# Key and query pieces of the attention layer: one product of 512 columns for the upper weights, and a sum afterwards

## The chip, the core and the metric

The kernel runs on one core of a Trainium2 chip. The core has a matrix engine (TensorE, PE in the profile, with its weight loads as PEld), a vector engine (VectorE, DVE), an activation engine (ScalarE, ACT), a general engine (GpSimd, POOL) and DMA queues, here issued from SyncE (SP). The time is the device time of one execution in microseconds (us); lower is better.

## The reference

A two-layer encoder trunk over 256 tokens of width 2048 in float32. Layer 0 mixes tokens with a convolution module, layer 1 with latent attention; each is followed by an MLP of width 8192. The change lies in the attention of layer 1:

```python
def mla(h, cos, sin, w_in, q_norm_g, kv_norm_g, w_q_up, w_kv_up, w_o):
    down = h @ w_in
    c_q, c_kv, k_pe = jnp.split(down, [Q_LORA_RANK, Q_LORA_RANK + KV_LORA_RANK], axis=-1)   # 512, 512, 64
    q = (rms_norm(c_q, q_norm_g) @ w_q_up).reshape(B, S, N_HEADS, QK_NOPE_DIM + QK_ROPE_DIM)
    q_nope, q_pe = jnp.split(q, [QK_NOPE_DIM], axis=-1)              # 128, 64 for each of 16 heads
    kv = (rms_norm(c_kv, kv_norm_g) @ w_kv_up).reshape(B, S, N_HEADS, QK_NOPE_DIM + V_HEAD_DIM)
    k_nope, v = jnp.split(kv, [QK_NOPE_DIM], axis=-1)                # 128, 128
    ...   # rotary parts, masked softmax of (q_nope k_nope + q_pe k_pe) * scale, times v
    return o @ w_o
```

## The kernel before

**Precision by parts.** A float32 operand is split into an upper part (a copy to a shorter float format, `fp32r`) and a lower part (the operand minus its upper part). A product is three matmuls that add up in one PSUM tile: upper times upper, lower times upper, upper times lower. ACT makes every upper part, DVE nearly every lower part, so each split is an ACT instruction followed by a DVE instruction that waits for it. Weights are split this way after each load (`split_half`, L164 to L179: ACT L170, DVE L174), one half of a unit at a time.

**Attention.** `kvh`/`kvl` and `qh`/`ql` hold the two parts of the normed compressed key/value and query, turned so that the 512 compressed channels lie on partitions in four blocks (`j` of `NJ` = 4) and the 256 tokens are columns. They are made by `to_T` from `ckv` and `cq` (ACT L209, DVE L216), for the query after `squares` (ACT L1502) and `normed` (DVE L1508). The 16 heads come in four groups of four. Work of a group is cut into pieces:

- `k_piece` and `qn_piece` (four of each in a group, one for each head): 12 matmuls of 256 columns, L1535 to L1537 and L1564 to L1566, into one PSUM tile, then `in_parts`: ACT makes the upper part (L209) and DVE the lower part (L214) of the 128 x 256 result, both from PSUM.
- `v_piece` (four): six matmuls of 512 columns; DVE copies the finished tile (L1552).
- `qp_piece` (two): the rotary part of the query; ACT copies it (L1579), POOL rotates it (`rope`, L1380 to L1385), and a few pieces later ACT and POOL split it (`qp_parts`: ACT L209 writing `qhl`, POOL L1599). `qp_turn` transposes it on PE (L1606), and ACT copies it out (L1615, L1616).

For each head, `scores` multiplies query and key parts on PE (10 matmuls), DVE takes the row maximum (L1651, L1652), ACT the exponential (L1654), and `weights` scales on DVE (L1661, L1664). `weights_turn` transposes on PE (L1670) with an ACT copy (L1672), `values` multiplies by v on PE (L1679, L1680) and splits the result into `oh` (ACT L209) and `ol` (DVE L214).

**Order.** The whole stage stands under a manual schedule: each engine's instructions run in the order in which the Python code issues them, and an instruction that waits holds up all that follows on its engine. The order is written out by hand. Before the heads: key pieces of group 0, value pieces, `to_T` of the query, `qp` and `qn` pieces of group 0, then three `qn` pieces of group 1, two `qp_turn`s, one more `qn` piece and a `qp` piece. Then the loop over heads; while group g is attended, the pieces of group g + 1 are made, and in the last group the output products `o_piece` run instead:

```python
scores(h)
piece(todo.pop(0))
weights(h)
prefetch(1)
piece(todo.pop(0))
if h > 0:
    weights_turn(h - 1)
if i > 1 and g + 1 < NG:
    qp_turn(g + 1, i - 2)
if h > 1:
    values(h - 2)
prefetch(1)
for w in todo:
    piece(w)
    prefetch(1)
```

`prefetch` splits a half of the weights that lie two units ahead (`LOOK`); a unit is the weights of four key, four query or four value pieces (two rotary ones), and its halves are 128 x 1024 (128 x 512 for the rotary ones). PSUM holds six tiles `acc` in rotation, one for each piece, score and value product, and two tiles `tr` for transposes.

Of the kernel before, what the change touches and what calls it, by code (L numbers as in the profile page):

```python
# [10 lines left out]
F32 = mybir.dt.float32  # L11
F32R = mybir.dt.float32r
BF16 = mybir.dt.bfloat16
I32 = mybir.dt.int32
AF = mybir.ActivationFunctionType
ALU = mybir.AluOpType
AX = mybir.AxisListType

P = 128
# [3 lines left out]
S = T * P  # L23
# [6 lines left out]
DN = 128  # L30
DR = 64
DV = 128
QR = 512
KR = 512
# [45 lines left out]
def trunk_kernel(  # L80
# [26 lines left out]
    nc = tc.nc  # L107
# [32 lines left out]
    def nm(s):  # L140
        uid[0] += 1
        return f"{s}_{uid[0]}"


    def acc_tile():
        return psum["acc"].tile([P, NB], F32, tag="acc", name=nm("acc"))
# [60 lines left out]
    def hi_part(ps, hi, scale=1.0):  # L207

        nc.scalar.activation(hi, ps, AF.Copy, scale=scale)  # L209

    def lo_part(ps, hi, lo, scale=None):

        if scale is None:
            nc.vector.tensor_tensor(lo, ps, hi.bitcast(F32), op=ALU.subtract)  # L214
        else:
            nc.vector.scalar_tensor_tensor(  # L216
                out=lo, in0=ps, scalar=scale, in1=hi.bitcast(F32), op0=ALU.mult, op1=ALU.subtract
            )
# [97 lines left out]
    at, cols = 0, []  # L316
# [441 lines left out]
    with ExitStack() as cx:  # L758
# [49 lines left out]
        def conv_w(n, j):  # L808
            half = raws[n].shape[1] // 2
            hi, lo = wjs[n, j // half]  # L810
            return hi[:, j % half, :], lo[:, j % half, :]
# [182 lines left out]
        with tc.manual_schedule():  # L994
# [273 lines left out]
            for m in range(NP):  # L1268
# [4 lines left out]
                for j in range(2):  # L1273
                    k = 2 * m + j
                    wh, wl = conv_w(NU + m, j)
# [4 lines left out]
                    for g, group in enumerate(groups):  # L1280
# [3 lines left out]
                        for b, t in order:  # L1284
                            bs = slice(b * NB, (b + 1) * NB)
                            for i, (x_kt, w) in enumerate(group):
                                nc.tensor.matmul(  # L1287
                                    ps2[b][t], x_kt(k, t), w[:, bs], start=k == g == i == 0,
                                    stop=k == KC - 1 and i == len(group) - 1,
# [4 lines left out]
                for q in {NP - 3: (0, 1, 4), NP - 2: (5, 2, 3), NP - 1: (6, 7)}.get(m, ()):  # L1294
                    t, i = divmod(q, NNB)
# [74 lines left out]
    with ExitStack() as cx:  # L1370
        at = cx.enter_context(tc.tile_pool(name="at", bufs=1, reuse_waits="tile"))
        at2 = cx.enter_context(tc.tile_pool(name="at2", bufs=2, reuse_waits="tile"))
# [18 lines left out]
        NJ = 4  # L1391
# [37 lines left out]
        raws, parts = {}, {}  # L1429
# [15 lines left out]
        def w_at(key, j):  # L1445
            n = pieces[key]
            half = units[n][1][1] // 2
            hi, lo = parts[n, j // half]
            return hi[:, j % half, :], lo[:, j % half, :]

        def start_unit(key, h):

            n = pieces[key]
            pending.append((n + LOOK, h))
# [10 lines left out]

        pad_kv = at.tile([P, PAD_KV], F32, name="pad_kv")
        nc.gpsimd.memset(pad_kv, 0.0)
        kvh = at.tile([P, KR // P, S], F32R, name="kvh")
        kvl = at.tile([P, KR // P, S], F32R, name="kvl")
        qh = at.tile([P, QR // P, S], F32R, name="qh")  # L1470
        ql = at.tile([P, QR // P, S], F32R, name="ql")

# [43 lines left out]
        def parts_tile(tag):  # L1518
            return [gp[0].tile([P, HG, S], F32R, tag=tag + c, name=nm(tag + c)) for c in "hl"]

        def in_parts(o, parts, i):
            hi_part(o, parts[0][:, i, :])
            lo_part(o, parts[0][:, i, :], parts[1][:, i, :])

        def k_piece(g, i):
            key = ("k", g)
            if i == 0:
                kTs[g] = parts_tile("kT")
            if i % 2 == 0:
                start_unit(key, i // 2)  # L1530
            o = acc_tile()[:, :S]
            ns = slice(i * DN, (i + 1) * DN)
            for j in range(NJ):
                wh, wl = w_at(key, j)
                nc.tensor.matmul(o, wh[:, ns], kvh[:, j, :], start=j == 0, stop=False)  # L1535
                nc.tensor.matmul(o, wh[:, ns], kvl[:, j, :], start=False, stop=False)  # L1536
                nc.tensor.matmul(o, wl[:, ns], kvh[:, j, :], start=False, stop=j == NJ - 1)  # L1537
            in_parts(o, kTs[g], i)

        def v_piece(g, t, half):  # L1540
# [13 lines left out]
        def qn_piece(g, i):  # L1554
            key = ("qn", g)
            if i == 0:
                qTs[g] = parts_tile("qT")
            if i % 2 == 0:
                start_unit(key, i // 2)
            o = acc_tile()[:, :S]  # L1560
            ns = slice(i * DN, (i + 1) * DN)
            for j in range(NJ):
                wh, wl = w_at(key, j)
                nc.tensor.matmul(o, wh[:, ns], qh[:, j, :], start=j == 0, stop=False)  # L1564
                nc.tensor.matmul(o, wh[:, ns], ql[:, j, :], start=False, stop=False)  # L1565
                nc.tensor.matmul(o, wl[:, ns], qh[:, j, :], start=False, stop=j == NJ - 1)  # L1566
            in_parts(o, qTs[g], i)

        def qp_piece(g, t):
# [48 lines left out]
        def kv_work(g):  # L1618
            return [lambda i=i: k_piece(g, i) for i in range(HG)] + [
                lambda t=t, half=half: v_piece(g, t, half) for t in range(T) for half in range(2)  # L1620
            ]

        def q_work(g):
            qn = [lambda i=i: qn_piece(g, i) for i in range(HG)]
            qp = [lambda t=t: qp_piece(g, t) for t in range(T)]
            return qn + qp if g == 1 else qp + qn
# [73 lines left out]
        with tc.manual_schedule():  # L1700
# [23 lines left out]
            for k in range(KC):  # L1724
                u, j = divmod(k, 2)
# [23 lines left out]
            for k in range(KC):  # L1749
                u, j = divmod(k, 4)  # L1750
# [3 lines left out]
                wh, wl = w_at(("q", u), j)  # L1754
# [189 lines left out]
```

## Time and profile before

| | |
|---|---|
| median of 3 runs | 1934.31 us (1934.09 to 1934.44) |
| the profiled execution | 1934.31 us, of which 1932.5 us span from first to last instruction |
| granted TensorE clock, mean | 0.999 |
| the stretch from the key pieces of group 0 to the first output product | from 1034.9 to 1143.0 us of the span |
| matmuls of key and query pieces | 6 lines x 64 = 384, of 256 columns each |

The page gives, for each engine, the time in which it had an instruction under way. On PE successive matmuls overlap, so the row says how much of the time PE was occupied and not how fast it went; the distance from one matmul's start to the next is the time that one takes up. The timeline gives the start and the length of each instruction. On ACT and DVE, too, the next instruction can start a little before the one ahead of it has ended; where it needs the result, it starts after its end.

### The profile page before, as it was taken

What the parts mean: (1) busy time and instruction counts of PE and PEld (TensorE: products, weight loads), DVE (VectorE), ACT (ScalarE), POOL (GpSimd) and SP (SyncE); (2) the same over time, 40 slices, a digit from 0 to 9 for tenths busy, and PEclk for the clock granted to TensorE, in tenths of its full rate; (3) what the DMA queues carried; (4) which work ended last, traced back from release to release, by engine and by line L of the source; (5) the groups of instructions that cost most, each with busy time, mean ns of one, the idle gap of its engine ahead of it and who ended that gap; (6) DMA issues with size and microseconds to landing.
All of it is one profiled execution on the core that took longest, in us unless ns stands there. A gap on an engine that the chain in (4) does not pass through costs nothing.

```text
span 1932.5 us, 28477 instructions
## 1 busy us (share of the span) xinstructions
PE 1921.0 (99%) x10725; PEld 1681.5 (87%) x10725; DVE 1592.2 (82%) x2457; ACT 1095.6 (57%) x1636; POOL 249.0 (13%) x208
## 2 busy tenths in 40 slices
PE   9999999999999999999999999999999999999998
PEld 8999888888888888888898998888888888888887
DVE  7999988877999776799976766877789987678998
ACT  5667755554555545555576655555555554455554
POOL 6999200000010100000001420000000010000000
PEclk9999999999999999999999999999999999999999
DMA  7766456665585866655656545465646776665774
GB/s 230 214 183 189 153 189 206 193 194 177 175 251 194 263 195 187 194 174 196 217 176 175 142 134 192 155 216 186 188 162 225 222 248 212 191 196 175 231 219 150
DMA packets 230427, 375.50 MB, mean 194 GB/s; under 512 B 16392, under 2 KB 107792, under 8 KB 230032
## 3 DMA queue, kind: packets, MB, share of 16 engines
q1 hardware_dynamic: 224640, 363.28, 58.7%
q0 software_dynamic: 4320, 7.87, 2.2%
q10 hardware_dynamic: 1328, 2.52, 0.4%
q8 instruction: 84, 1.38, 0.3%
q14 instruction: 55, 0.45, 0.1%
HBM read 363.68 MB, written 2.10 MB: 189 GB/s over the span
## 4 chain that ended last, share of the span: by engine, by line
PE 97%; DVE 2%; DMA 0%; ACT 0%; issue 0%; ACTq 0%; DVEq 0%
PE acc L655 24%; PE acc L205 15%; PE acc L203 15%; PE acc L204 15%; PE acc L656 13%; PE acc L823 8%; PE acc L1287 2%; DVE sum L910 1%; DMA xs<-in_x 0%; PE acc L1535 0%; PE acc L1566 0%; PE acc L1565 0%; PE acc L1536 0%; PE acc L1564 0%; PE acc L1537 0%; PE tr L267 0%
## 5 line engine op out<-in xcount | busy, mean ns | idle before, releaser
L174 DVE TENSOR_TENSOR lo<-raw,hi 128x1024 fp32r<-128x1024 f32 (+2 forms) x509 | 602.2, 1197 | 232.3 <-ACT hi L170 226.6
L170 ACT ACTIVATE hi<-raw 128x1024 fp32r<-128x1024 f32 (+2 forms) x574 | 583.9, 1036 | 361.1 <-PE acc L655 203.7
L655 PE MATMUL acc<-xt,hi 128*128 128x512 f32 x2048 | 710.6, 390 | 0.0
L656 PE MATMUL acc<-xt,lo 128*128 128x256 f32 x2048 | 577.5, 282 | 0.0
L655 PEld LDWEIGHTS acc<-xt,hi 128*128 128x128 f32 x2048 | 384.3, 188 | 80.7
L656 PEld LDWEIGHTS acc<-xt,lo 128*128 128x128 f32 x2048 | 387.1, 189 | 0.2
L497 ACT ACTIVATE hi<-raw 128x1024 fp32r<-128x1024 f32 x248 | 228.7, 948 | 228.3 <-DVE raw L505 134.0
L498 DVE TENSOR_TENSOR lo<-raw,hi 128x1024 fp32r<-128x1024 f32 x248 | 263.9, 1087 | 27.6 <-ACT hi L497 22.5
L203 PE MATMUL acc<-hi,sh 128*128 128x512 f32 x514 | 200.1, 389 | 0.0
L205 PE MATMUL acc<-lo,sh 128*128 128x512 f32 x514 | 200.1, 389 | 0.0
L203 PE MATMUL acc<-hi,gh 128*128 128x512 f32 (+1 forms) x516 | 200.0, 388 | 0.0
L205 PE MATMUL acc<-lo,gh 128*128 128x512 f32 (+1 forms) x516 | 199.9, 387 | 0.0
L204 PE MATMUL acc<-hi,gl 128*128 128x512 f32 (+1 forms) x516 | 199.9, 387 | 0.0
L823 PE MATMUL acc<-xt,hi 128*128 128x256 f32 x1024 | 180.2, 281 | 0.3 <-ACT b L1106 0.2
L204 PE MATMUL acc<-hi,sl 128*128 128x512 f32 x450 | 175.1, 389 | 0.0
L578 POOL DMA_DIRECT2D xs<-v x30 | 26.5, 994 | 1136.4 <-DVE lo L174 703.2
L910 DVE SCALAR_TENSOR_TENSOR sum<-ub,w_dw,sum 128x256 f32<-128x256 f32 x409 | 164.3, 481 | 3.6 <-ACT sum L880 3.0
L174 POOL TENSOR_TENSOR lo<-raw,hi 128x1024 fp32r<-128x1024 f32 x65 | 155.0, 2410 | 17.3 <-ACT hi L170 17.3
L823 PEld LDWEIGHTS acc<-xt,hi 128*128 128x128 f32 x1024 | 154.8, 188 | 1.1 <-ACT xt L1090 0.6
L823 PE MATMUL acc<-xt,lo 128*128 128x256 f32 x512 | 139.2, 279 | 0.0
L205 PEld LDWEIGHTS acc<-lo,sh 128*128 128x128 f32 x514 | 96.5, 188 | 20.4 <-DVE lo L498 0.3
L204 PEld LDWEIGHTS acc<-hi,gl 128*128 128x128 f32 x516 | 96.9, 188 | 19.9
(314 smaller groups left out, 2531.3 us busy)
## 6 DMA issues: line engine op xcount, KB each, us to landing
raw<-in_mlp_w SPq DMA_DIRECT2D x255, 1024.0 KB, 5.5
raw<-in_conv_w_pw SPq DMA_DIRECT2D x62, 512.0 KB, 5.1
raw<-in_conv_w_pw SPq DMA_DIRECT2D x16, 1024.0 KB, 5.1
raw<-in_mla_w_o SPq DMA_DIRECT2D x16, 1024.0 KB, 5.7
raw<-in_mla_w_kv_up SPq DMA_DIRECT2D x32, 256.0 KB, 3.9
xs<-v POOLq DMA_DIRECT2D x30, 256.0 KB, 7.8
raw<-in_mla_w_in SPq DMA_DIRECT2D x8, 576.0 KB, 3.8
raw<-in_mla_w_in SPq DMA_DIRECT2D x4, 1024.0 KB
```

The costliest lines, as they stand in the source:

```text
L170: nc.scalar.activation(hi, raw[:, js, :], AF.Copy)
L174: eng.tensor_tensor(lo, raw, hi.bitcast(F32), op=ALU.subtract)
L203: nc.tensor.matmul(ps, sh, mh, start=start, stop=False)
L204: nc.tensor.matmul(ps, sl, mh, start=False, stop=False)
L205: nc.tensor.matmul(ps, sh, ml, start=False, stop=stop)
L497: nc.scalar.activation(hi, src, AF.Copy)
L498: nc.vector.tensor_tensor(lo, src, hi.bitcast(F32), op=ALU.subtract)
L655: nc.tensor.matmul(ps[b], wh[:, bs], xhl(k), start=k == 0, stop=False)
L656: nc.tensor.matmul(ps[b][:, :S], wl[:, bs], xh(k), start=False, stop=k == KC - 1)
L823: nc.tensor.matmul(pss[c][b][:, :S], w[i][:, bs], (xh, xl)[j](k), start=k == i + j == 0, stop=end and k == k0 + nk - 1 and (i, j) == terms ...
L910: nc.vector.scalar_tensor_tensor(out=out, in0=ubs[c][:, w : w + S], scalar=tap(c, w), in1=base, op0=ALU.mult, op1=ALU.add)
L1287: nc.tensor.matmul(ps2[b][t], x_kt(k, t), w[:, bs], start=k == g == i == 0, stop=k == KC - 1 and i == len(group) - 1,)
```

## The change

`kvh` and `kvl` become the two halves of one tile `kvhl` of 512 columns for each block `j`, and `qh` and `ql` those of `qhl`. In a key or query piece the upper weights are multiplied by all 512 columns in one matmul, into a whole PSUM tile: its left half gets upper times upper, its right half upper times lower. The lower weights are multiplied by the upper half of the input into the left half. So a piece is four matmuls of 512 columns and four of 256 in place of twelve of 256. The two halves of the PSUM tile are then added: ACT copies the right half to a new tile `two` in SBUF (two buffers), DVE adds the left half, and upper and lower parts are made from that tile, not from PSUM.

```diff
-        kvh = at.tile([P, KR // P, S], F32R, name="kvh")
-        kvl = at.tile([P, KR // P, S], F32R, name="kvl")
-        qh = at.tile([P, QR // P, S], F32R, name="qh")
-        ql = at.tile([P, QR // P, S], F32R, name="ql")
+        kvhl = at.tile([P, KR // P, 2 * S], F32R, name="kvhl")
+        qhl = at.tile([P, QR // P, 2 * S], F32R, name="qhl")
+        (kvh, kvl), (qh, ql) = ([a[:, :, :S], a[:, :, S:]] for a in (kvhl, qhl))
...
+        def two_widths(o, w_j, ns, src, low):
+            for j in range(NJ):
+                wh, wl = w_j(j)
+                nc.tensor.matmul(o, wh[:, ns], src[:, j, :], start=j == 0, stop=False)
+                nc.tensor.matmul(o[:, :S], wl[:, ns], low[:, j, :], start=False, stop=j == NJ - 1)
+
         def in_parts(o, parts, i):
-            hi_part(o, parts[0][:, i, :])
-            lo_part(o, parts[0][:, i, :], parts[1][:, i, :])
+            v = at2.tile([P, S], F32, tag="two", name=nm("two"))
+            nc.scalar.activation(v, o[:, S:], AF.Copy)
+            nc.vector.tensor_tensor(v, o[:, :S], v, op=ALU.add)
+            hi_part(v, parts[0][:, i, :])
+            lo_part(v, parts[0][:, i, :], parts[1][:, i, :])
...   # in k_piece; qn_piece likewise with qhl, qh
-            o = acc_tile()[:, :S]
-            ns = slice(i * DN, (i + 1) * DN)
-            for j in range(NJ):
-                wh, wl = w_at(key, j)
-                nc.tensor.matmul(o, wh[:, ns], kvh[:, j, :], start=j == 0, stop=False)
-                nc.tensor.matmul(o, wh[:, ns], kvl[:, j, :], start=False, stop=False)
-                nc.tensor.matmul(o, wl[:, ns], kvh[:, j, :], start=False, stop=j == NJ - 1)
+            o = acc_tile()
+            two_widths(o, lambda j: w_at(key, j), slice(i * DN, (i + 1) * DN), kvhl, kvh)
             in_parts(o, kTs[g], i)
```

More of the change, by code (lines that the diff above doesn't have):

```diff
@@ L1559, in qn_piece @@
                 start_unit(key, i // 2)
[L1560 to L1566, printed above, removed]
+            o = acc_tile()
+            two_widths(o, lambda j: w_at(key, j), slice(i * DN, (i + 1) * DN), qhl, qh)
             in_parts(o, qTs[g], i)
```

## The prediction, made before the changed kernel was built or run

> **What bounds the kernel now.** The page first: which engine is full, and which carries the chain that ended last.
>
> ```profile
> span 1932.5 us, 28477 instructions
> PE 1921.0 (99%) x10725; PEld 1681.5 (87%) x10725; DVE 1592.2 (82%) x2457; ACT 1095.6 (57%) x1636; POOL 249.0 (13%) x208
> PE 97%; DVE 2%; DMA 0%; ACT 0%; issue 0%; ACTq 0%; DVEq 0%
> ```
>
> PE is occupied throughout and makes 97% of the chain, so time is saved only by fewer PE cycles, and lost wherever PE comes to wait. Next, the changed stretch: engines by window (length; then busy us of PE, PEld, DVE, ACT, POOL), and the waits between engines.
>
> ```profile
> 1049.00:1064.00 15.00, 15.00 (x131) 15.00 (x130) 8.71 (x13) 11.96 (x25) 9.41 (x14) 1.00 0.64 175
> 1095.00:1124.00 29.00, 29.00 (x222) 27.67 (x221) 20.76 (x47) 18.67 (x49) 10.04 (x16) 1.00 0.51 149
> ACT pr L1654 <- DVE mx L1652: 23.6, 13, 2.7
> ```
>
> The second window is one group of four heads. PE never waits in it; DVE has 8.2 us of idle time, ACT 10.3. But much of ACT's idle time is of one kind: it stands at the exponential until DVE has the maximum (23.6 us over the stage). ACT and DVE run in the code's order, so idle time is usable only where the next instruction's input is there. That is what the change has to be measured against.
>
> **What PE gains.** Starts in the timeline, of key pieces (three matmuls of 256 columns per block) and of the MLP's first product, which has the new form (512, then 256):
>
> ```profile
> 1034.91 0.28 PE L1535 MATMUL acc<-kvh,hi 128*128 128x256 f32 x1
> 1040.51 0.39 PE L203 MATMUL acc<-hi,kvh 128*128 128x512 f32 x1
> 330.02 0.39 PE L655 MATMUL acc<-xt,hi 128*128 128x512 f32 x1
> 333.84 0.39 PE L655 MATMUL acc<-xt,hi 128*128 128x512 f32 x1
> L1535 PE MATMUL acc<-kvh,hi x64: 277/280/364, 1034.9 to 1131.9; 128*128 128x256 f32 x64
> ```
>
> Four key pieces, 16 threes, lie between the first two rows: 5.60 / 16 = 0.350 us. Between the next two lie 11 pairs: 3.82 / 11 = 0.347. Both are 768 columns, and the time goes by columns. The change replaces 32 pieces x 4 = 128 threes: 128 x 0.0027 = **0.35 us gained**. The 128 weight loads that go were hidden behind matmuls. The 0.280 us of a matmul (last row) isn't its price: three of those would be 0.84 us, and the starts are 0.350 apart.
>
> **What ACT and DVE are given.** Each of 32 pieces gets a copy and an add of 128 x 256, and its parts then come from SBUF. The MLP has the same copy and add:
>
> ```profile
> L673 ACT ACTIVATE v<-acc x128: 362/384/387, 321.7 to 1760.5; 128x256 f32<-128x256 f32 x128
> L674 DVE TENSOR_TENSOR v<-acc,v x128: 414/420/426, 322.1 to 1761.1; 128x256 f32<-128x256 f32 x128
> 1103.04 0.38 ACT L209 ACTIVATE kTh<-acc 128x256 fp32r<-128x256 f32 x1
> 1103.30 0.64 ACT L170 ACTIVATE hi<-raw 128x512 fp32r<-128x512 f32 x1
> 1103.45 0.42 DVE L214 TENSOR_TENSOR kTl<-acc,kTh 128x256 fp32r<-128x256 f32 x1 [1.32 <-ACT kTh L209]
> 1103.80 0.15 DVE L1661 RECIPROCAL zs<-zs 128x2 f32<-128x2 f32 x1
> L686 ACT ACTIVATE gh<-v x32: 612/616/634, 348.8 to 1763.9; 128x512 fp32r<-128x512 f32 x32
> L687 DVE TENSOR_TENSOR gl<-v,gh x32: 682/684/686, 350.1 to 1765.5; 128x512 fp32r<-128x512 f32 x32
> ```
>
> Copy 0.38, add 0.42. An instruction that doesn't need the last one's result starts earlier than that one ends (ACT 1103.04, then 1103.30: a step of 0.27; DVE's 0.42 has a step of 0.34); one that crosses engines starts 0.03 us after the end (1103.42, 1103.45). Reading the parts from SBUF isn't in this trace at 256 columns in this form. The last two rows have it at 512; half of that, 0.31 and 0.34, bounds it below (a gain against the old 0.38 and 0.42), the whole above. As an instruction has a fixed share, 0.40 and 0.41 are taken, near the old ones.
>
> As work this fits: 8 pieces a group add 8 x 0.42 = 3.4 us to DVE and 3.1 to ACT. As order it doesn't. A piece had one crossing, ACT to DVE; ACT went on at once. Now ACT copies, DVE adds, ACT must wait for the add before the upper part, and everything behind it waits too: the splits of weights, exponentials, copies of transposes. DVE's add in turn stands behind the weights' lower part of 1.2 us that the last split queued. A piece's **link** in that alternating chain is add 0.42 + 0.04, upper part 0.30 (its step), next copy 0.38 + 0.04: 1.18 us. A large half of weights between two pieces puts in 1.05 + 0.03 for its upper part and 1.14 for the lower one's step, less the 0.41 in which the next copy runs: 1.81; a small half likewise 0.62 + 0.03 + 0.60 - 0.41 = 0.84. PE's piece is 1.39. I walked both queues by these durations from the key pieces to the output products. The same walk with the old pieces keeps PE fed throughout and puts the first output product at 1142.0, where the trace has 1142.96 (its row is below).
>
> **Front: query input late, 3.1 us.**
>
> ```profile
> 1037.07 0.36 ACT L209 ACTIVATE kTh<-acc 128x256 fp32r<-128x256 f32 x1
> 1037.33 0.62 ACT L170 ACTIVATE hi<-raw 128x512 fp32r<-128x512 f32 x1
> 1037.98 0.69 DVE L174 TENSOR_TENSOR lo<-raw,hi 128x512 fp32r<-128x512 f32 x1
> 1038.92 0.16 DVE L259 TENSOR_SCALAR ms<-sq 128x2 f32<-128x2 f32 x1
> 1040.18 0.88 DVE L1508 TENSOR_SCALAR cq<-cq,y 128x512 f32<-128x512 f32 x2
> 1043.51 0.69 DVE L1552 COPY vv<-acc 128x512 f32<-128x512 f32 x1
> 1044.82 1.66 DVE L216 SCALAR_TENSOR_TENSOR ql<-tr,vecs,qh 128x256 fp32r<-128x256 f32 x4 [0.62 <-ACT qh L209]
> 1046.98 0.28 PE L203 MATMUL acc<-hi,qh 128*128 128x256 f32 x1
> ```
>
> From the first copy at 1037.05: copy 0.42, add 0.45, upper 0.30, half 0.66 + 0.60; second piece's add and parts 0.45 + 0.44 + 0.33; the norm's six small steps 1.26 (1038.92 to 1040.18) and scaling 0.80; third piece 0.45 + 0.30, half 0.66 + 0.60; fourth 0.45 + 0.30; large half 1.09 + 1.14; value copy 0.60; four `ql` 1.63; crossing 0.03. Sum 12.96: 1050.01. PE is there at 1046.98 less 0.1, and **stands 3.1 us**. The lower parts used to end half a microsecond ahead of PE; that cover is gone.
>
> **Eight query pieces in a row, 3.6 us, and heads 0 to 3, 5.1 us.**
>
> ```profile
> 1050.03 2.94 DVE L174 TENSOR_TENSOR lo<-raw,hi 128x1024 fp32r<-128x1024 f32 x2 [1.71 <-ACT hi L170]
> 1057.67 1.28 ACT L244 ACT_TABLE_LOAD   x1
> 1059.62 1.04 PE L1606 MATMUL tr<-ident,qhl 128*128 128x128 f32 x8
> 1061.29 0.59 ACT L1616 ACTIVATE qpB<-tr 64x512 fp32r<-64x512 f32 x1
> 1063.61 0.27 PE L1648 MATMUL acc<-kpA,qpA 128*128 128x128 f32 x1
> ```
>
> DVE, 3.1 us late and two large lower parts behind, makes the first add at 1055.52. Then seven links less the first copy 7.84, two small halves 1.68, a large one 1.81, two `qhl` steps 0.62, table load and warm-up 1.40, `qpA` and `qpB` 1.07: `qpB` is there at 1069.9. The transposes of `qp_turn` wait 0.7 for `qhl`, which stands behind the pieces; then `scores(0)` stops at its fourth matmul, due at 1063.61 + 3.1 + 0.7 = 1067.4 (1067.0 in the walk, whose pieces are shorter), until `qpB`: **3.0**. Over heads 0 to 3, whose queues start late, the walk has three stands more: the first key piece of group 1 for its weights (1.93), the turn of head 1 (1.72), and a `qp_turn` whose PSUM tile waits for an ACT copy (1.43): **5.1**.
>
> **Groups 1 and 2, 15.5 us, and the end, 1.1.**
>
> ```profile
> 1095.61 0.33 PE tr L1670 x3
> 1103.34 0.33 PE tr L1670 x3
> 1132.39 0.33 PE tr L1670 x3
> 1101.33 0.60 DVE L1651 TENSOR_REDUCE mx<-acc 128x1 f32<-128x128 f32 x2
> 1101.97 0.17 DVE L1652 TENSOR_SCALAR mx<-mx 128x2 f32<-128x2 f32 x1
> 1102.23 0.37 ACT L1654 ACTIVATE pr<-acc,mx 128x128 f32<-128x128 f32 x1 [2.04 <-DVE mx L1652]
> 1104.09 0.51 ACT L1672 ACTIVATE pT<-tr 128x384 f32<-128x384 f32 x1
> 1142.96 0.39 PE L203 MATMUL acc<-hi,oh 128*128 128x512 f32 x1
> ```
>
> In the chain of waits head 5, with two query and two key pieces, is 7.73 us of PE (1095.61 to 1103.34), and a whole group 29.05. Head 5 from its maximum to the next head's, on ACT and DVE: maximum to end of exponentials 1.66 (1.71 in the rows, 1101.33 to 1103.04); copy, add, upper part 1.17, `qhl` 0.31, large half's upper 1.08; its lower 1.14, add 0.46, upper 0.30, `pT` 0.37, `oh` 0.27; copy 0.38, `ol` 0.09, add 0.46, upper 0.30, small half 0.65; its lower 0.60, add 0.46, upper 0.43, lower 0.33. **10.46**, so this chain and no longer PE sets the pace. By the same links heads 4 to 11 take 10.2, 10.5, 9.3, 6.1, 10.2, 11.4, 9.8, 6.1: 73.6, where PE needs 2 x 29.05 = 58.1. Excess **15.5**; and the first output product stands 1.1 more for a PSUM tile that a value copy frees. After that no such piece is left and PE leads again. The loads of weights on SP follow the splits that free their buffers, so they come as late as those; each is issued three units, some 17 us of PE's work, before its use, which takes the delay of some 3 to 5 us.
>
> **Sum.** 3.1 + 3.6 + 5.1 + 15.5 + 1.1 - 0.35 = **+28.1 us**. The profiled execution was 1934.31 us (span 1932.5 and 1.8 around it), which is also the median, so **1962.4 us**. Bounds: with copy, add and upper part at their steps (0.27, 0.34, 0.30) the walk gives +23; with crossings of 0.09 (1102.14 to 1102.23 in the maximum's rows) +34. The likeliest case's own range is 1955 to 1970.
>
> **Rivals.** A measurement of this kernel tells 0.2%, 3.9 us, from no change.
>
> *The extra work hides.* For it: the idle shares above, and PE that never waited. Then only the 0.35 us is left: 1934.0. Against: the links. Chance 0.07.
>
> *Only the unbroken runs stall.* If heads absorb their pieces (splits taken while ACT would wait at the exponential anyway), 3.1 + 3.6 - 0.35 remain: 1940.7. Against: the chain above counts those waits as passed. Chance 0.10.
>
> *Fewer matmuls pay by their own length.* Two lengths of 0.39 and 0.28 for three of 0.28 would save 0.17 x 128 = 21.5 us: 1912.8, faster. It decides if pairs start more than 0.1 us closer than threes; the rows say 0.003. The Trainium skill's "Perfetto Trace Analysis", section "Matmuls", calls larger matmuls more efficient, which speaks for this; the starts above bear it out by 0.8% only. Chance 0.05.
>
> *PE slows after standing.* Five stands of the walk are about 2.6 to 3.3 us. If the two pieces after each took twice their 1.39, that is 5 x 2.8 = 14 us more: 1976. The rows here grant a clock of 1.00 throughout and show no such stand, so they decide nothing. The skill's "TensorE: Matmul & The Clock Gate", section "Why this matters for your kernels", has the clock halve after a gap of some 3 us; by that rule the longest stands would just reach it. Chance 0.08.
>
> The forecast keeps 0.70. Range 1946 to 1976: it holds the likeliest case, the slowed clock, and part of the way to the second rival. Faster 0.05, within 0.2% 0.07, slower 0.88.
>
> **What would show it.** Right: the new 512 and 256 matmuls start 0.347 us a pair apart; PE busy falls by some 25 us in the attention stretch, with waits of PE named ACT (`qpB`, `pT`) and DVE (`ql`, the add, weights' lower part); ACT's longest new wait is at the upper parts of `two` for the add; the output products start near 1170 instead of 1143; the stages after are only shifted. Wrong: PE without idle time there, or ACT and DVE instructions in another order than the code's.

## The result, and the profile after

The changed kernel takes **1964.06 us** (median of 4 runs, 1963.63 to 1966.34), the one before 1934.28: a ratio of 1.0156, 95% interval 1.0139 to 1.0174, 29.8 us slower. The forecast was 1962.4. The profiled execution took 1963.63 us, with a span of 1961.8.

The page of the changed kernel, and its windows over the attention stage (length; busy us of PE, PEld, DVE, ACT, POOL; granted clock; share of the DMA engines and GB/s):

```profile
span 1961.8 us, 28288 instructions
PE 1931.7 (98%) x10597; PEld 1681.8 (86%) x10597; DVE 1607.3 (82%) x2489; ACT 1108.2 (56%) x1668; POOL 249.1 (13%) x208
PE 92%; DVE 4%; ACT 2%; issue 1%; DMA 1%; SPq 0%; ACTq 0%; DVEq 0%
...
1064.00:1095.00 31.00, 24.30 (x133) 21.52 (x132) 20.44 (x46) 18.82 (x47) 9.59 (x14) 0.84 0.38 106
1095.00:1128.00 33.00, 30.66 (x195) 27.10 (x194) 21.52 (x49) 20.18 (x54) 9.85 (x14) 1.00 0.31 83
1128.00:1166.00 38.00, 31.73 (x188) 27.03 (x187) 25.39 (x54) 22.17 (x57) 10.02 (x14) 0.96 0.35 111
1166.00:1212.00 46.00, 45.59 (x227) 38.59 (x228) 26.19 (x51) 23.86 (x49) 0.00 (x0) 0.96 0.49 159
```

The first of these windows in the kernel before:

```profile
1064.00:1095.00 31.00, 31.00 (x240) 29.68 (x240) 23.96 (x54) 20.30 (x54) 16.39 (x22) 1.00 0.47 130
```

PE, never idle in this stage before, now is, and 5 points of the chain have gone from PE to DVE, ACT, DMA and the gaps between them. No engine is full: in the first of the changed kernel's windows DVE has 20.4 busy us of 31 and ACT 18.8. Their busy time over the whole run rose by 15 and 13 us, the added instructions. The seventh number is new: a granted clock of 0.84 where it had been 1.00.

Who waited for whom in the stage, PE's own waits first (total us, times, longest):

```profile
PE tr L1670 <- ACT pT L1672: 5.1, 2, 2.9
PE tr L1670 <- DVE pr L1664: 2.6, 1, 2.6
PE acc L1648 <- ACT qpA L1615: 2.5, 1, 2.5
PE acc L204 <- DVE qhl L216: 1.5, 1, 1.5
PE acc L1525 <- DVE two L1531: 1.5, 2, 1.3
PE tr L1606 <- ACT pT L1672: 1.4, 1, 1.4
PE tr L1606 <- POOL qhl L1599: 1.3, 1, 1.3
...
ACT qTh L209 <- DVE two L1531: 16.9, 16, 1.6
ACT kTh L209 <- DVE two L1531: 15.1, 16, 1.7
```

Each of the 32 upper parts makes ACT wait for the add, 32 us in all. PE's waits are behind those: for the turned weights, the query's copies and parts, freed PSUM tiles. The first output product starts late by as much as the whole run, so the rest is only shifted:

```profile
1172.16 0.39 PE L203 MATMUL acc<-hi,oh 128*128 128x512 f32 x1
```

That is 29.2 us after the 1142.96 of before.

### The profile page after: what moved, and what is told of

The parts are those of the page before. It is cut to its first block, busy times and chain, and to the rows that moved or that the text cites. A ratio compares the mean times of both kernels' runs of the same rounds, so it can differ in the third digit from the quotient of the medians.

```text
span 1961.8 us, 28288 instructions
## 1 busy us (share of the span) xinstructions
PE 1931.7 (98%) x10597; PEld 1681.8 (86%) x10597; DVE 1607.3 (82%) x2489; ACT 1108.2 (56%) x1668; POOL 249.1 (13%) x208
## 4 chain that ended last, share of the span: by engine, by line
PE 92%; DVE 4%; ACT 2%; issue 1%; DMA 1%; SPq 0%; ACTq 0%; DVEq 0%
PE acc L655 24%; PE acc L203 14%; PE acc L205 14%; PE acc L204 14%; PE acc L656 13%; PE acc L823 8%; PE acc L1287 2%; DVE sum L910 1%; DVE lo L174 1%; ACT hi L170 1%; DVE two L1531 1%; DMA raw<-in_mla_w_kv_up 0%; DMA xs<-in_x 0%; PE tr L267 0%; ACT pr L1654 0%
## 5 line engine op out<-in xcount | busy, mean ns | idle before, releaser
L205 PEld LDWEIGHTS acc<-lo,sh 128*128 128x128 f32 x514 | 96.5, 188 | 20.4 <-DVE lo L498 0.3
L205 PEld LDWEIGHTS acc<-lo,gh 128*128 128x128 f32 x516 | 96.9, 188 | 19.9
```

The source lines that it names most:

```text
L205: nc.tensor.matmul(ps, sh, ml, start=False, stop=stop)
```

## The experiments

Times are medians, with the kernel before beside them on the same chip. Edits are against the changed kernel unless said otherwise. Two expectations count the runs in the order in which they were made: their "second run" is experiment 3 here, their "sixth run" experiment 7.

**1. The products alone.**

```diff
         def in_parts(o, parts, i):
-            v = at2.tile([P, S], F32, tag="two", name=nm("two"))
-            nc.scalar.activation(v, o[:, S:], AF.Copy)
-            nc.vector.tensor_tensor(v, o[:, :S], v, op=ALU.add)
-            hi_part(v, parts[0][:, i, :])
-            lo_part(v, parts[0][:, i, :], parts[1][:, i, :])
+            hi_part(o[:, :S], parts[0][:, i, :])
+            lo_part(o[:, :S], parts[0][:, i, :], parts[1][:, i, :])
```

> Only the new form of the products: each key and query piece is four matmuls of 512 and four of 256 columns, and its parts are made straight from the left half of the PSUM tile as before. Copy and add are left out, and with them the term upper weights times lower input. Theory of order (ACT and DVE made to wait for each other in turn cost the time): PE's gain of 0.35 us alone is left, 1933.9. Theory of work (the added instructions fill DVE and ACT): the same, 1933.9. Theory of the products (the wide product into a whole PSUM tile itself slows PE or its tiles): it stays near 1964.

1933.82 us against 1934.25 (ratio 0.9998, 0.9989 to 1.0007). The 0.4 us less is what the columns promised, and it lies inside the interval. The new products cost nothing that can be measured and bring next to nothing.

**2. The old products, with copy and add.**

```diff
             for j in range(NJ):
                 wh, wl = w_j(j)
-                nc.tensor.matmul(o, wh[:, ns], src[:, j, :], start=j == 0, stop=False)
+                if j == 0:
+                    nc.tensor.matmul(o, wh[:, ns], src[:, j, :], start=True, stop=False)
+                else:
+                    nc.tensor.matmul(o[:, :S], wh[:, ns], low[:, j, :], start=False, stop=False)
+                    nc.tensor.matmul(o[:, S:], wh[:, ns], src[:, j, S:], start=False, stop=False)
```

> The old products of 256 columns (the 512 form is left for the first of four blocks only, where it opens both halves), aimed at the two halves of the tile, with copy, add and parts as in the change. Theory of order and theory of work: the loss is all here, 1964. Theory of the products: back to about 1934 to 1941.

1964.19 us (1.0155, 1.0142 to 1.0169): the whole loss, and its trace has the same waits of ACT for the add, 16.9 and 15.1 us. It is all in copy, add and what hangs on them; whether as work or as order this run cannot tell.

**3. The same work, set apart: a first attempt.**

```diff
-            v = at2.tile([P, S], F32, tag="two", name=nm("two"))
+            u, v = (at2.tile([P, S], F32, tag=f"two{c}", name=nm("two"), bufs=1) for c in range(2))
             nc.scalar.activation(v, o[:, S:], AF.Copy)
-            nc.vector.tensor_tensor(v, o[:, :S], v, op=ALU.add)
-            hi_part(v, parts[0][:, i, :])
-            lo_part(v, parts[0][:, i, :], parts[1][:, i, :])
+            nc.vector.tensor_tensor(u, o[:, :S], kpA.bitcast(F32), op=ALU.add)
+            hi_part(o[:, :S], parts[0][:, i, :])
+            lo_part(o[:, :S], parts[0][:, i, :], parts[1][:, i, :])
```

> The new products, and the same added work on ACT and DVE, but nothing waits for it: ACT copies the right half of the PSUM tile to one SBUF tile, DVE adds the left half to a tile that has long been written, neither result is used, and the parts come straight from PSUM. The term upper weights times lower input is left out. Theory of order: no alternation, so within 2 us of before, 1934 to 1936 (walking the queues gives at most +3.6). Theory of work: as with the change, about 1964.

1960.61 us (1.0137, 1.0121 to 1.0152). By the numbers that is the theory of work. The waits of its trace say otherwise:

```profile
ACT qTh L209 <- DVE two L1531: 16.2, 16, 1.5
ACT kTh L209 <- DVE two L1531: 14.9, 16, 1.7
...
DVE two L1531 <- ACT two L1530: 12.0, 8, 2.3
```

No result passes between these instructions, and still ACT waits for DVE 32 times: they read the same PSUM tile, and the program's semaphores, from which the profile infers its waits, keep such readings in order. The Trainium skill's "PSUM — Partial Sum Buffer", section "PSUM bank collisions raise a hardware error", says that two engines must not touch the same partitions of a bank at the same time, readers included; the rows fit that. So the alternation had stayed, and the run tells nothing against the theory of order.

**4. The same work on SBUF.** The edit against experiment 3:

```diff
-            nc.scalar.activation(v, o[:, S:], AF.Copy)
-            nc.vector.tensor_tensor(u, o[:, :S], kpA.bitcast(F32), op=ALU.add)
+            nc.scalar.activation(v, kpA.bitcast(F32), AF.Copy)
+            nc.vector.tensor_tensor(u, kpA.bitcast(F32), kpA.bitcast(F32), op=ALU.add)
             hi_part(o[:, :S], parts[0][:, i, :])
             lo_part(o[:, :S], parts[0][:, i, :], parts[1][:, i, :])
```

> The second run's question again, with nothing to wait for: its copy and add both read the PSUM tile, and the trace shows each made to wait for the other engine's reading of it, so the alternation had stayed. Here the same two instructions of 128 x 256 in each piece (copy on ACT, add on DVE) read and write SBUF tiles that no other engine touches, and the parts come straight from PSUM; the sum, and the term upper weights times lower input, are left out. Theory of order: the added work alone is hidden, 1934 to 1936. Theory of work: about 1960 or more.

1938.64 us against 1934.12 (1.0023, 1.0014 to 1.0033). The same number of instructions of that size costs 4.8 us over the first experiment's 1933.82, more than the 2 expected, and far from 30. Window, and PE's longest waits in the stage:

```profile
1095.00:1128.00 33.00, 32.42 (x209) 29.16 (x208) 26.09 (x58) 22.98 (x61) 13.17 (x17) 1.00 0.45 132
...
PE acc L1525 <- DVE qTl L214: 1.5, 2, 1.0
PE tr L1670 <- DVE pr L1664: 1.2, 1, 1.2
```

DVE carries 26.1 us in 33 here, more than with the change (21.5), and PE is busy for 32.4 of the 33. Fullness was not what held the changed kernel.

**5. The change, with a piece's parts issued one piece later.**

```diff
             nc.scalar.activation(v, o[:, S:], AF.Copy)
             nc.vector.tensor_tensor(v, o[:, :S], v, op=ALU.add)
-            hi_part(v, parts[0][:, i, :])
-            lo_part(v, parts[0][:, i, :], parts[1][:, i, :])
+            parts_now()                      # upper and lower parts of the piece before
+            parts_due.append((v, parts, i))
...   # parts_now() is also called ahead of value and rotary pieces
```

> The change with one thing moved: copy and add of a piece are issued where they were, but its upper and lower parts are issued one piece later, behind the copy and add of the next piece (or ahead of the next value or rotary piece). The same work, and ACT hardly ever meets an add that isn't done. Theory of order: most of the loss goes, 1936 to 1941 (walking the queues gives +4 to +8). Theory of work: stays at about 1964.

1941.46 us (1.0037, 1.0024 to 1.0051), 0.5 us above the range. Nothing is left out, the instructions are the same, and **22.6 of the 29.8 us are gone**. Between ACT and DVE the stage keeps its other waits, but ACT's 32 waits for an add, 32 us in the change, are now two of 0.7 us together:

```profile
ACT pr L1664 <- DVE mx L1662: 30.1, 16, 2.6
DVE two L1531 <- ACT two L1530: 14.4, 12, 2.6
...
ACT kTh L209 <- DVE two L1531: 0.7, 2, 0.6
```

**6. The change, with the upper part made by DVE.**

```diff
-            hi_part(v, parts[0][:, i, :])
+            nc.vector.tensor_copy(parts[0][:, i, :], v)
```

> The change with the upper part of a piece made by DVE behind its own add, not by ACT: ACT gives the copy and goes on, and nothing comes back to it. DVE has one instruction of 128 x 256 more for each of 32 pieces, some 12 us in all, ACT as much less. Theory of order: the crossing back to ACT is what costs, so a large part goes, 1940 to 1947 (walking the queues gives +9 to +13). Theory of work (DVE is the one that is full): slower than the change, above 1966.

1949.03 us against 1934.01 (1.0078, 1.0063 to 1.0093). Half the loss goes although DVE gets more to do. The time is 2 us above the range expected. DVE is now busy for 26.8 us of the 33 from 1095 on, where the change had 21.5, and ACT waits for its maximum nearly twice as long as with the change (26.0 us there):

```profile
ACT pr L1654 <- DVE mx L1652: 48.3, 16, 4.3
```

That DVE's own row of instructions is what remains is read from these rows; no run shows it apart, nor from the low clock, which came up here too, once, after a stand of 2.9 us.

**7. Does the low clock cost time of its own?** Transposes that nobody reads, ahead of the long stands.

```diff
+            if h == 0:
+                dummies(h, 22)               # transposes into unused columns of head h's score tile
...
+                        dummies(h, {2: 25, 7: 22, 11: 29}.get(h, 0))
                         weights_turn(h - 1)
+                    if h == 2:
+                        dummies(h, 13)
```

> The change with transposes of the identity into unused columns of a score tile, put on PE just ahead of the four long stands (22 ahead of head 0's scores, 25 and 13 around head 2's turn, 22 and 29 ahead of the turns of heads 7 and 11; 0.11 us each, some 12 us of PE where it would stand). If the clock that falls after those stands costs time of its own: the granted clock stays at 1.00 in the stage and the time falls by up to the 7.7 us that PE's groups run longer at the low clock, to 1956 to 1961. If ACT and DVE set the pace anyway and the slow matmuls lie in their shadow: the clock stays up and the time stays within 2 us of 1964.

1985.05 us (1.0261, 1.0244 to 1.0278), off on both readings. The waits show why:

```profile
PE acc L1663 <- ACT pr L1656: 22.0, 3, 8.0
```

L1663 is the added transpose: in heads 2, 7 and 11 it waited for the exponential on ACT, which reads the same PSUM tile. So the run tested that wait and not the clock.

**8. The same into the tile of the coming value product.**

```diff
+                    n = {2: 25, 7: 22, 11: 29}.get(h, 0)
+                    if n:
+                        val[h - 2] = acc_tile()
+                        dummies(val[h - 2][:, 3 * P :], n)
...   # head 2's other 13 go to the same tile; values(h) takes its tile from val
```

> The sixth run's question again: its transposes went to score tiles that ACT was still reading, and each waited for ACT up to 8 us, so it tested that wait and not the clock. Here they go to the PSUM tile of the value product that comes next, which nothing reads yet (head 0's stay in its own score tile ahead of the scores). If the low clock after the long stands costs time of its own: granted clock near 1.00 in the stage and 1956 to 1961. If slow matmuls lie in the shadow of ACT and DVE: clock near 1.00 and 1962 to 1966.

1961.59 us (1.0142, 1.0127 to 1.0157). The two windows where the changed kernel had 0.84 and 0.96, and PE's longest wait in the stage:

```profile
1064.00:1095.00 31.00, 29.78 (x204) 26.39 (x203) 20.29 (x45) 18.90 (x48) 9.60 (x14) 1.00 0.38 108
1128.00:1166.00 38.00, 33.43 (x217) 29.15 (x217) 25.37 (x54) 22.18 (x57) 10.02 (x14) 1.00 0.35 109
...
PE acc L1525 <- DVE two L1531: 4.0, 3, 1.4
```

The clock stays at 1.00, and 2.5 us go, of the 7.7 that experiment 7's expectation names. The time falls between the two ranges, 0.4 us below that of the shadow. The intervals of the two ratios overlap (1.0139 to 1.0174 with the change), so 2.5 us is little more than the noise. The rows do show a shadow: where PE no longer works slowly it stands instead, 4.0 us for the add where it stood 1.5 with the change. The added transposes may hold PE up a little themselves; no run tells by how much.

The steps from kernel to kernel: products -0.4 (experiment 1); added work with nothing to wait for +4.8 (4 against 1); the alternation +23.0 (8 against 4); the low clock +2.5 (the change against 8). Each step starts where the last one ended, so that they add up to the loss proves nothing. Experiment 4 takes the parts from PSUM and 8 adds PE work, so the single terms are good to a few us only. The 22.6 us that experiment 5 gives back are an independent measure of the third.

## Why the prediction was right, and where its parts were not

**The price of the products** held. The 16 pairs of the first four key pieces start 0.347 us apart (1034.60 to 1040.15), as forecast, and experiment 1 gained 0.4 us where 0.35 was forecast. The rival that matmuls pay by their length (1912.8) is out.

**Durations.** The trace of the change has what had to be borrowed:

```profile
L1530 ACT ACTIVATE two<-acc x32: 359/366/414, 1036.8 to 1163.3; 128x256 f32<-128x256 f32 x32
L1531 DVE TENSOR_TENSOR two<-acc,two x32: 409/418/427, 1037.2 to 1164.6; 128x256 f32<-128x256 f32 x32
L209 ACT ACTIVATE kTh<-two x16: 416/418/420, 1037.6 to 1165.1; 128x256 fp32r<-128x256 f32 x16
L214 DVE TENSOR_TENSOR kTl<-two,kTh x16: 424/426/618, 1038.1 to 1165.5; 128x256 fp32r<-128x256 f32 x16
```

Taken were 0.38, 0.42, 0.40 and 0.41, all within 0.02 us of these medians.

**The chain of head 5** can be read off, DVE's rows first:

```profile
1111.05 0.62 DVE L1651 TENSOR_REDUCE mx<-acc 128x1 f32<-128x128 f32 x2
1113.18 0.42 DVE L1531 TENSOR_TENSOR two<-acc,two 128x256 f32<-128x256 f32 x1 [1.32 <-ACT two L1530]
1115.45 1.21 DVE L174 TENSOR_TENSOR lo<-raw,hi 128x1024 fp32r<-128x1024 f32 x1
1116.58 0.41 DVE L1531 TENSOR_TENSOR two<-acc,two 128x256 f32<-128x256 f32 x1
1118.47 0.41 DVE L1531 TENSOR_TENSOR two<-acc,two 128x256 f32<-128x256 f32 x1
1120.50 0.42 DVE L1531 TENSOR_TENSOR two<-acc,two 128x256 f32<-128x256 f32 x1
1121.74 0.62 DVE L1651 TENSOR_REDUCE mx<-acc 128x1 f32<-128x128 f32 x2
...
1117.03 0.42 ACT L209 ACTIVATE qTh<-two 128x256 fp32r<-128x256 f32 x1 [1.44 <-DVE two L1531]
1118.92 0.42 ACT L209 ACTIVATE kTh<-two 128x256 fp32r<-128x256 f32 x1 [0.55 <-DVE two L1531]
```

From maximum to maximum 1121.74 - 1111.05 = 10.69 us, forecast 10.46. The add at 1116.58 stands behind the weights' lower part of 1.21 us, and ACT's 1.44 us of idle time is its wait for that add, as the walk had it. Experiments 2, 4 and 5 show that this order is the cause and not only goes with the loss: copy and add in this order bring the whole loss back without the new products, as much work with nothing to wait for costs 4.8 us, and with the parts put off by a piece 22.6 us come back.

**The front was over-sized.** Forecast 3.1 us, and the profile has 1.5:

```profile
1048.13 1.65 DVE L216 SCALAR_TENSOR_TENSOR qhl<-tr,vecs,qhl 128x256 fp32r<-128x256 f32 x4
1048.66 0.39 PE L204 MATMUL acc<-hi,qhl 128*128 128x256 f32 x1 [1.51 <-DVE qhl L216]
```

The step that failed is "four `ql` 1.63": PE went on after the first of the four lower parts, as its first block needs only that one. The sum up to there was right (the four begin at 1048.13, by the forecast's walk at 1048.35). The stand of 1.93 us at group 1's first key piece is not in the trace either: PE is at half clock there and the weights come in time. With the clock kept up (experiment 8) PE stands for them, but less, and only at the third of four blocks:

```profile
1074.60 0.38 PE L1526 MATMUL acc<-kvhl,lo 128*128 128x256 f32 x1 [0.76 <-DVE lo L174]
```

Nor does the trace have the 1.1 us ahead of the first output product. Together these terms were some 4.6 us too much. The loads of weights were covered nearly as forecast: DVE waits for one twice in the stage, 0.9 us in all.

**Heads 0 to 3 were under-sized.** PE's own rows place the loss, the kernel before first, then the changed one:

```profile
1087.71 0.49 PE L1670 MATMUL tr<-ident,pr 128*128 128x128 f32 x3
1069.46 0.33 PE L1648 MATMUL acc<-kpA,qpA 128*128 128x128 f32 x1 [2.53 <-ACT qpA L1615]
1102.70 0.49 PE L1670 MATMUL tr<-ident,pr 128*128 128x128 f32 x3
```

The fourth matmul of head 0's scores, at 1063.61 before, is 5.9 us late, where the first two terms made 6.7 (it waits for `qpA`; the forecast named `qpB`, which ACT makes next). The transposes of head 3's weights (its turn, L1670) are 15.0 late: heads 0 to 3 cost 9.1 us where 5.1 were forecast. From there to the first output product 14.2 us come on top, where 16.6 were forecast. In heads 0 to 3 lie two of the four falls of the clock (10 us at half clock in all); with the clock kept up (experiment 8) the same turn starts at 1100.46, 2.2 us sooner. The stands by themselves are longer than forecast, too (head 1's turn 2.6 for 1.72).

**The clock was left out of the sum** and stood as a rival at 0.08. It fell: the windows above lose 0.16 x 31 + 0.04 x 38 + 0.04 x 46 = 8.3 us of full clock. The rival's mechanism was right and its size was not: 14 us more were forecast, and experiment 8 finds 2.5, the rest lying in the shadow of ACT and DVE. One of the forecast's signs missed for this reason: PE's busy time was to fall by some 25 us in the stage and fell by 18.5.

```profile
1034.00:1172.00 138.00, 119.51 (x694) 103.81 (x693) 91.52 (x196) 84.24 (x208) 38.78 (x56) 0.94 0.39 113
```

Of the 29.2 us, 18.5 are PE standing and up to 8.3 PE working slowly; these rows do not place the rest.

So the total of 28.1 against 29.8 is nearer than its parts: over-sized terms and an under-sized one with the clock in it partly cancelled. That much of the agreement is luck; the pace set by ACT and DVE, its largest term, is not.

**Work hides** (1934.0) was wrong as a whole, but nearly right of the work: experiment 4 has it at 4.8 us. That **only the unbroken runs stall** (1940.7) fell with head 5's rows above and with the 14.2 us lost after head 3.

## What to carry to other kernels

Before moving an operation to an engine that has idle time, ask what that engine waits for and what stands behind it: in this kernel a step that went from one in-order engine to another and back cost some 23 us where the same work without the crossing cost 5, and busy shares did not show it. Where the detour is needed, issue the return step one unit of work later, so that its input is there when its turn comes. Price a matmul in a full pipeline by the distance between starts (0.347 us for a pair here), not by the length in its row (0.39 and 0.28).

## What the hardware showed that was not expected

- Two engines that only read the same PSUM tile were kept apart by waits (experiment 3: 32 waits of ACT, 31 us, with no data passed), and matmuls into unused columns of such a tile waited for its reader (experiment 7, up to 8.0 us).
- PE's four longest stands with the change, 2.2 to 2.9 us, were each followed by a halved TensorE clock for 3.4 to 6.9 us (another stand, of 1.4 us, lies in the longest); the one of 1.5 us was not. In experiment 3 one of 2.0 us was, and one of 1.7 us was not. One window at half clock, from the change:

```profile
1090.00:1093.00 3.00, 3.00 (x14) 2.82 (x13) 1.75 (x6) 2.70 (x8) 0.00 (x0) 0.50 1.04 300
```

The Trainium skill's "TensorE: Matmul & The Clock Gate", section "Why this matters for your kernels", puts the limit at about 3 us of idle time; here it was less.
